# Gate products written to PSUM in the order of their eviction, and one more low one-hot group on ACT

## The chip, the cores and the metric

The kernel runs on one core of a Trainium2 chip. Its engines work side by side and wait for each other by semaphores: PE (TensorE, matrix products into PSUM), ACT (ScalarE), DVE (VectorE), POOL (GpSimd), and SP, whose queue issues the DMA transfers between DRAM and SBUF. The metric is the time of one execution on the device in microseconds (us); what is compared is the median over several runs.

## The reference

A trunk of two layers over 256 latent tokens with 256 context tokens as a prefix, 1024 features. Each layer has an attention mixer and then an expert network, PEER, whose routing the change touches:

```python
def blk(xb):                                  # 128 tokens
    q = (xb @ wq).reshape(PEER_TBLOCK, PEER_HEADS, 2, PEER_DQ // 2)
    s = jnp.einsum('thpd,pnd->thpn', q, sub_keys).astype(jnp.float32)
    sv, si = lax.top_k(s, PEER_TOPK)
    cand = (sv[:, :, 0, :, None] + sv[:, :, 1, None, :]).reshape(...)
    cidx = (si[:, :, 0, :, None] * PEER_NKEYS + si[:, :, 1, None, :]).reshape(...)
    fv, fp = lax.top_k(cand, PEER_TOPK)
    eidx = jnp.take_along_axis(cidx, fp, axis=-1)
    g = jax.nn.softmax(fv, axis=-1)
    ue = jnp.take(u, eidx, axis=0)
    ve = jnp.take(v, eidx, axis=0)
    a = jnp.einsum('thkd,td->thk', ue, xb).astype(jnp.float32)
    wgt = (jax.nn.gelu(a, approximate=False) * g).astype(xb.dtype)
    return jnp.einsum('thk,thkd->td', wgt, ve)
```

Each token has 8 heads with 16 experts each, so 128 pairs (i, j) of half keys with a gate g; the expert is 128 i + j of 16384.

## The kernel before

**Dense experts.** For most token blocks (three of four in layer 0, two of two in layer 1) the kernel does not gather rows. It goes through all 16384 experts in 128 chunks: `achunk` forms the activations of one chunk for all tokens (a product of the tokens with u, split in a high and a low part, lines 191 to 193, or in plain float32, line 213; then Gelu on ACT, line 1023, into a ring buffer), `weight` multiplies them with the gates (line 1151), and `fchunk` multiplies the result with v. For this the gates must lie as a dense matrix G[i, j, token], zero where a token does not choose an expert. `gates` builds it, and it is `gates` that the change touches.

**Building G.** For one token the 128 x 128 matrix of gates is a product of two one-hot matrices over its 128 choices: `oh` (choice k has j) and `og` (choice k has i, times its gate). Per block of 128 tokens there are 16 builds of 8 tokens, so 48 builds in layer 0 and 32 in layer 1. One build does the following.

- DVE writes both one-hot matrices in float16 (line 930, `oh`).
- The gate goes into `og` as a high and a low float16 part. The high part is one DVE instruction (line 933). The low part has four groups of two tokens: the first `d = 4 - AGRP` groups are one DVE instruction (line 936), of the others each token is one ACT activation of 128 columns (line 940). With `AGRP = (2,)` it is two groups on DVE, and 4 activations.
- GPIPE = 2 builds later PE forms the products (line 954): 8 tokens, two products each (high and low part, accumulated), in two PSUM tiles `p` of four tokens.
- ACT copies each tile, scaled, to `stage` (line 957), the eviction. `stage` holds 32 tokens in the order [i, token], so that the token is innermost. The tile in PSUM lies as [token, i]: the eviction reads it in a row and writes each word 32 words (128 bytes) behind the last.
- After every fourth build SP writes `stage` to G in DRAM (two transfers, line 961). When all is written, `load_g` reads G back in pieces for the main loop (line 1139).

**The order.** The code is a set of generators: `prologue` steps through the routing and the builds, and between steps `peer` puts in chunks of `achunk`, 27 ahead in layer 0 and 47 in layer 1 (`LAG`), and in layer 0 pieces of the next layer's modulation vectors (`filler`; weights of line 162, products of line 245). The tile layer then orders the instructions of each engine by its own reckoning of when they can start; on the chip each engine runs its list in order. The stages that hold the builds I call the gate stages.

Of the kernel before, what the change touches and what calls it, by code (L numbers as in the profile page):

```python
# [34 lines left out]
KLAG = 3  # L35
AGRP = (2,)
YLAG = (3, 3)
# [38 lines left out]
class Phase:  # L76
    """a pool whose tags have a set number of buffers"""

# [12 lines left out]
class Kernel:  # L91
# [32 lines left out]

# [1 line left out]
    def start_weights(self):  # L126
# [60 lines left out]

# [1 line left out]
    def mm3(self, out, lh, ll, rh, rl, start, stop):  # L189
# [5 lines left out]
    def proj_t(self, key, hh, hl, c=512, **kw):  # L195
        """[128 columns, c tokens] in PSUM"""
        if key in self.pre:
            return self.pre.pop(key)
        w = self.take(key, **kw)
        p = self.ps()  # L200
        if not isinstance(w, tuple):
            self.product8(p[:, :c], w)
            return p
        wh, wl = w
        for k in range(8):
            b = slice(k * 128, (k + 1) * 128)
            self.mm3(p[:, :c], wh[:, b], wl[:, b], hh[:, k, :c], hl[:, k, :c], k == 0, k == 7)
        return p

    def product8(self, out, w):  # L210
        """the same in float32, of the modulated norm kept whole"""
        for k in range(8):
            self.nc.tensor.matmul(out, w[:, k * 128:(k + 1) * 128], self.h32[:, k, :], start=k == 0, stop=k == 7)  # L213

    def proj_n(self, name, hh, hl, width, nt=4):
        """natural layout: nt banks [128 tokens, width]"""
        ps = [self.ps() for _ in range(nt)]
        for b in range(4):
            wh, wl = self.take((name, b))
            for q in range(2):  # L220
                c = slice(q * width, (q + 1) * width)
                for t in range(nt):
                    tt = slice(t * 128, (t + 1) * 128)
                    self.mm3(ps[t][:, :width], hh[:, 2 * b + q, tt], hl[:, 2 * b + q, tt],
                             wh[:, c], wl[:, c], b == 0 and q == 0, b == 3 and q == 1)
        return ps
# [3 lines left out]

# [1 line left out]
    def ada_mm(self, l, v, half, pool):  # L232
        """half of one modulation vector for both conditions, in rows 0 and 1 of each 32 as four partial sums"""
        nc = self.nc
# [69 lines left out]

# [1 line left out]
    def rstd(self, ss, n, width):  # L306
# [7 lines left out]
    def squares(self, x, half, ss, junk):  # L314
        """sum of squares of one half of a token block; with the second the factor of the norm"""
        self.nc.scalar.activation(junk, x[:, half * 512:half * 512 + 512], AF.Square, accum_out=ss[:, half:half + 1])
        if half:
            s = self.small([128, 1], "ss1")
            self.nc.vector.tensor_tensor(s, ss[:, 0:1], ss[:, 1:2], op=OP.add)
            return self.rstd(s, 1, D)  # L320

    def norm_mod(self, xs, rst, l, vsh, vsc, keys, mid=None):
        """modulated norm, transposed; the projections of keys go along with it"""
        nc = self.nc
# [51 lines left out]
    def rope(self, x, p, perm, cos, sin, n):  # L376
        """x [128, n] from p in PSUM, its first 256 columns (the latents) rotated, the rotation after the next one"""
        self.nc.scalar.copy(x[:, :n], p[:, :n])
        self.rope_end()
        self.roping = (x, perm, cos, sin)  # L380
# [13 lines left out]

# [1 line left out]
    def out_proj(self, l, yh, yl, src, T):  # L396
# [38 lines left out]

# [1 line left out]
    def probs1(self, P, S, scale, sink=None, bias=None):  # L437
        """P [128, 2, nk] <- exp of the two heads' scores less their maximum; sums in sm"""
        nc = self.nc
# [30 lines left out]
    def flip(self, x, nk, eng):  # L470
        """[128, 128 nk] -> [128 keys, nk, 128]"""
        p = self.ps([128, nk, 128])
        for k in range(nk):
            self.transpose(p[:, k, :], x[:, k * 128:(k + 1) * 128])
        t = self.m.t("PT", [128, nk, 128])
        if eng:
            self.nc.vector.tensor_copy(t, p)
        else:
            self.nc.scalar.copy(t, p)
        return t  # L480

# [1 line left out]
    def mixer0(self, xs, sq):  # L483
# [99 lines left out]

# [1 line left out]
    def mixer1(self, xs, sq):  # L585
# [9 lines left out]
        self.rope(kr, self.proj_t(("cdin", 0), hh, hl), *r32, 512)  # L595
        # cq | ckv in natural layout
        ckv = self.proj_n("ckv", hh, hl, 384)
# [36 lines left out]
        nc.vector.tensor_tensor(kvl, kf, kvh.bitcast(F), op=OP.subtract)  # L634
        # kr (replicated), dq, dk transposed
        dq, dk = [], []
# [13 lines left out]
        for t, p in enumerate(self.proj_n("dv", hh, hl, 512)):  # L650
            self.rope_end()
            nc.scalar.copy(dv[t // 2][:, t % 2, :], p)
        # latent queries, keys and values
        wh, wl = self.take(("uq", 0))
# [121 lines left out]

# [1 line left out]
    def top16(self, V, X, a, b):  # L778
        """sorted top 16 of each a, b as scratch, interleaved over the lists"""
        nc = self.nc  # L780
# [11 lines left out]
    def route_scores(self, l, T, nd, hh, hl):  # L792
        """sorted top 16 of each half key for the dense blocks; scores of a further block go to DRAM"""
        nc = self.nc
# [43 lines left out]
    def route(self, sv, al):  # L838
        """experts i, j and gates of one token block; a generator, leaves them in self.rt"""
        nc = self.nc  # L840
# [63 lines left out]
    def gates(self, go, ti, G):  # L904
        """gate matrix of 128 tokens -> DRAM; a generator"""
        nc = self.nc
# [36 lines left out]
        def product():  # L943
# [5 lines left out]
            for half in range(2):  # L949
                p = self.ps([128, 4, 128])  # L950
                for k in range(4):
                    for w in range(2):
                        g, b = half * 2 + k // 2, k % 2
                        nc.tensor.matmul(p[:, k, :], oh[:, 0, g, :, b], og_[:, w, g, :, b], start=(w == 0),  # L954
                                         stop=(w == 1))
                c4 = q * 8 + half * 4
                nc.scalar.activation(stage[:, :, c4:c4 + 4].rearrange("p i t -> p t i"), p, AF.Copy,  # L957
                                     scale=1.0 / GSCALE)
            if q == 3:
# [12 lines left out]
    def peer(self, l, xs, sq, nd):  # L972
        """nd dense token blocks; a further block, if any, goes by gathered rows; returns the pieces of f"""
        nc = self.nc
# [49 lines left out]

        # routing and gate matrix, with the first products of the main loop in between
        def prologue():
# [71 lines left out]
        def gather(n0, n1, after=None):  # L1098
            """rows of slots n0..n1, not before after is there"""
            n1 = min(n1, 256)  # L1100
# [69 lines left out]
        def pace(j):  # L1170
            """slots used by the end of iteration j, even in time"""
            def at(i):
                return i + min(i, NCH - lag)
            return min(256, -(-256 * (at(j + 1) - at(LATE)) // (at(NCH - 3) - at(LATE))))
# [28 lines left out]
    def residual(self, l, f):  # L1203
        """x + g2 f, in a new mixer phase"""
        nc = self.nc
# [27 lines left out]
    def run(self):  # L1233
# [34 lines left out]
        nc.vector.tensor_scalar(self.nsink, self.pk("sink"), -1.0, None, op0=OP.mult)  # L1268
        # lambda of the differential heads, gain of its norm
        lv = self.const([128, 2], name="lv")  # L1270
# [28 lines left out]
        xs, sq = self.residual(1, f)  # L1299
        # final norm  # L1300
        fg = self.m.t("q4", [128, 1024], name="fg")
# [16 lines left out]

# [1 line left out]
def rope_table(dim):  # L1320
    """cos and sin of the axial rotation for one head of dim features, [dim, 256 positions]"""
    half = dim // 4
# [11 lines left out]
def rope_perm(dim):  # L1334
    """lhsT of the product that gives (-x2, x1) for each quarter pair, over 128 partitions"""
    q = dim // 4
# [8 lines left out]
def col_blocks(w):  # L1345
    """[1024, 128 n] -> [n, 128 rows of a block, 8 blocks * 128 columns]"""
    k, n = w.shape
    return np.ascontiguousarray(w.reshape(8, 128, n // 128, 128).transpose(2, 1, 0, 3)).reshape(n // 128, 128, 1024)


def row_pairs(w):
    """[1024, n] -> [4, 128, 2 * n]"""
    k, n = w.shape
# [3 lines left out]
def layout(x, c, ctx, c_ctx, ada_w, ada_b, norm1_g, norm2_g, w_out, peer_wq, peer_keys, peer_u, peer_v,  # L1357
# [55 lines left out]
    z["na_bias"] = nb  # L1413
    # layer 0 projections
    w = ab_w_in[0]
    pair = np.concatenate([np.concatenate([np.arange(64) + 64 * h, np.arange(64) + 64 * (h + 4)]) for h in range(4)])
    z["ab_in"] = col_blocks(np.concatenate([w[:, 0:1024], w[:, 1536 + pair], w[:, 2048:2304]], 1))
    z["ab_v"] = row_pairs(w[:, 1024:1536])
    # layer 1 projections
    w = cd_w_in[0]  # L1420
# [39 lines left out]
```

## Time and profile before

| | us |
|---|---|
| runs of the kernel before, median of 3 | 2739.52 |
| their lowest and highest | 2731.03, 2754.28 |
| the profiled execution, span from first to last instruction | 2734.2 |
| TensorE busy in it | 2610.7 |
| ACT busy in it | 1267.3 |

The profile is of one execution. For it the span is the time that is known, and nothing is known of what lies around it; it is within the range of the three runs, 5.3 us under their median. A busy engine in the profile is one that has an instruction in flight; products on TensorE overlap each other, so that a busy TensorE need not be a full one.

### The profile page before, as it was taken

The numbers are of one execution on the slowest core, as the hardware profiler recorded it, in microseconds if no ns is written. First come the engines' busy times: TensorE is split into PE (matmuls) and PEld (weight loads), VectorE is DVE, ScalarE is ACT, GpSimd is POOL, SyncE is SP. The second block draws the span as 40 slices with busy tenths as digits, with TensorE's granted clock in tenths as the row PEclk, the third lists the DMA queues.
The fourth block names the chain that finished last, engine by engine and source line by source line (L and its number), as shares of the span: only waits on it lengthen the run. The fifth ranks groups of instructions, "written<-read, shape, count | busy, mean of one in ns | idle before, by whom it ended". The sixth has DMA issues, their size and how long they took to land.

```text
span 2734.2 us, 43073 instructions
## 1 busy us (share of the span) xinstructions
PE 2610.7 (95%) x16265; PEld 2261.8 (83%) x16265; DVE 1876.3 (69%) x3862; ACT 1267.3 (46%) x2201; POOL 529.2 (19%) x534
## 2 busy tenths in 40 slices
PE   7999998989999999999999989998999999999998
PEld 6866787878899999999899767757999899999986
DVE  4267588886977777777777765365997565555455
ACT  3255335997333333333333333343499444444454
POOL 0000000000045555566565530000000000000000
PEclk9999999999999999999999998998999999999999
DMA  7262323977688888888888862453467976565355
GB/s 291 101 216 86 111 88 128 287 235 246 232 313 311 308 315 306 316 299 321 294 309 288 275 225 75 164 195 113 144 215 242 318 267 210 208 211 214 130 193 183
DMA packets 240977, 614.15 MB, mean 225 GB/s; under 512 B 18384, under 2 KB 102608, under 8 KB 240768
## 3 DMA queue, kind: packets, MB, share of 16 engines
q1 hardware_dynamic: 203904, 477.17, 50.6%
q0 software_dynamic: 36864, 134.23, 13.9%
q8 instruction: 127, 2.08, 0.3%
q14 instruction: 82, 0.67, 0.1%
HBM read 558.90 MB, written 52.43 MB: 224 GB/s over the span
## 4 chain that ended last, share of the span: by engine, by line
PE 62%; DVE 6%; DMA 3%; ACT 3%; issue 2%; POOL 1%; SPq 0%; DVEq 0%; POOLq 0%; ACTq 0%
PE p L192 19%; PE p L191 19%; PE p L193 19%; DMA gr<-in_v,ix 1%; PE p L213 1%; PE s L707 1%; PE p L229 1%; DVE ws L168 1%; ACT stage L957 1%; ACT og L940 1%; DVE vs L168 1%; DMA sc<-sd 1%; PE p L954 1%; ACT ws L167 1%; PE p L245 0%
## 5 line engine op out<-in xcount | busy, mean ns | idle before, releaser
L167 ACT CAST ws<-w 128x1024 fp32r<-128x1024 f32 (+1 forms) x327 | 343.0, 1050 | 634.0 <-PE p L192 581.4
L168 DVE TENSOR_TENSOR ws<-w,ws 128x1024 fp32r<-128x1024 f32 (+1 forms) x327 | 397.5, 1216 | 267.7 <-ACT ws L167 267.4
L192 PE MATMUL p<-vs,w 128*128 128x512 f32 x1280 | 502.2, 393 | 7.5 <-DVE vs L168 7.5
L167 ACT CAST vs<-v 128x1024 fp32r<-128x1024 f32 x256 | 269.5, 1053 | 509.5 <-PE p L192 509.5
L191 PE MATMUL p<-vs,w 128*128 128x512 f32 x1280 | 499.6, 391 | 4.4 <-ACT vs L167 4.4
L193 PE MATMUL p<-vs,w 128*128 128x512 f32 x1280 | 501.6, 392 | 0.0
L191 PE MATMUL p<-hh,ws 128*128 128x384 f32 (+2 forms) x1336 | 472.2, 354 | 6.2 <-ACT ws L167 2.9
L193 PE MATMUL p<-hh,ws 128*128 128x384 f32 (+2 forms) x1336 | 466.0, 349 | 1.5 <-DVE ws L168 1.5
L192 PE MATMUL p<-hl,ws 128*128 128x384 f32 (+2 forms) x1336 | 466.6, 349 | 0.0
L168 DVE TENSOR_TENSOR vs<-v,vs 128x1024 fp32r<-128x1024 f32 x256 | 312.8, 1222 | 152.7 <-ACT vs L167 151.0
L191 PE MATMUL p<-hp,ws 128*128 128x256 f32 x1032 | 295.5, 287 | 1.8 <-ACT ws L167 1.1
L193 PE MATMUL p<-hp,ws 128*128 128x256 f32 x1032 | 292.8, 284 | 0.8 <-DVE ws L168 0.8
L192 PE MATMUL p<-hp,ws 128*128 128x256 f32 x1032 | 293.2, 284 | 0.0
L192 PEld LDWEIGHTS p<-vs,w 128*128 128x128 f32 x1280 | 241.3, 189 | 56.5 <-DVE vs L168 11.1
L193 PEld LDWEIGHTS p<-vs,w 128*128 128x128 f32 x1280 | 240.9, 188 | 53.7 <-DVE w L1153 3.0
L191 PEld LDWEIGHTS p<-vs,w 128*128 128x128 f32 x1280 | 241.1, 189 | 50.6 <-ACT vs L167 4.6
L191 PEld LDWEIGHTS p<-hh,ws 128*128 128x128 f32 x1336 | 255.0, 191 | 24.7 <-ACT ws L167 4.3
L192 PEld LDWEIGHTS p<-hl,ws 128*128 128x128 f32 x1336 | 254.6, 191 | 14.9 <-issue 0.5
L193 PEld LDWEIGHTS p<-hh,ws 128*128 128x128 f32 x1336 | 254.5, 190 | 13.1 <-DVE ws L168 2.0
L1123 DVE SCALAR_TENSOR_TENSOR acc<-gr,ga,acc 128x1024 f32<-128x1024 f32 x128 | 164.2, 1283 | 102.3 <-DMA gr<-in_v,ix 101.7
L1118 DVE SCALAR_TENSOR_TENSOR gr<-gr,hn 128x1024 f32<-128x1024 f32 x128 | 156.2, 1224 | 108.5 <-DMA gr<-in_u,ix 102.5
L311 POOL TENSOR_TENSOR rso<-rsm,mhalf 128x1 f32<-128x1 f32 x30 | 20.1, 671 | 1079.4 <-DVE rsm L309 1079.4
(267 smaller groups left out, 4127.6 us busy)
## 6 DMA issues: line engine op xcount, KB each, us to landing
w<-in_uT SPq DMA_DIRECT2D x256, 512.0 KB
v<-in_v SPq DMA_DIRECT2D x256, 512.0 KB
w<-in_ada_w SPq DMA_DIRECT2D x96, 512.0 KB
G<-stage SPq DMA_DIRECT2D x40, 1024.0 KB
g<-G SPq DMA_DIRECT2D x32, 768.0 KB
w<-in_wq SPq DMA_DIRECT2D x32, 512.0 KB
g<-G SPq DMA_DIRECT2D x32, 512.0 KB
w<-in_w_out SPq DMA_DIRECT2D x16, 512.0 KB
```

The lines of the kernel that those rows point to most:

```text
L167: self.nc.scalar.copy(hi, raw)
L168: self.nc.vector.tensor_tensor(lo, raw, hi.bitcast(F), op=OP.subtract)
L191: m(out, lh, rh, start=start, stop=False)
L192: m(out, lh, rl, start=False, stop=False)
L193: m(out, ll, rh, start=False, stop=stop)
L213: self.nc.tensor.matmul(out, w[:, k * 128:(k + 1) * 128], self.h32[:, k, :], start=k == 0, stop=k == 7)
L229: self.nc.tensor.transpose(out, x, self.ck("ident"))
L707: nc.tensor.matmul(S[:, s, :], a[c][h, q], b[c][h, :], start=True, stop=kind == "d", tile_position=(64 * s, 0))
L940: nc.scalar.activation(og_[:, 1, g, :, b], oh[:, 1, g, :, b], AF.Copy, scale=gl[:, k:k + 1])
L954: nc.tensor.matmul(p[:, k, :], oh[:, 0, g, :, b], og_[:, w, g, :, b], start=(w == 0), stop=(w == 1))
L1118: nc.vector.scalar_tensor_tensor(t, t, 1.0, hn, op0=OP.mult, op1=OP.mult, accum_out=ga[:, 0, n:n + 1])
L1123: nc.vector.scalar_tensor_tensor(acc, t, ga[:, 0, n - 128:n - 127], acc, op0=OP.mult, op1=OP.add)
```

## The change

`AGRP` goes from 2 to 3: of the four low groups of a build three are on ACT (6 activations) and one on DVE (128x256 in place of 128x512). The PSUM tile `p` changes its order from [token, i] to [i, token]: each product writes its 128 words four words apart, four tokens lie interleaved, and the eviction reads PSUM in a row and writes runs of four words to `stage`, one run each 128 bytes. The rest of the diff takes out comments and moves lines behind 957 up by one.

```diff
-AGRP = (2,)
+AGRP = (3,)
...
             for half in range(2):
-                p = self.ps([128, 4, 128])
+                p = self.ps([128, 128, 4])
                 for k in range(4):
                     for w in range(2):
                         g, b = half * 2 + k // 2, k % 2
-                        nc.tensor.matmul(p[:, k, :], oh[:, 0, g, :, b], og_[:, w, g, :, b], start=(w == 0),
+                        nc.tensor.matmul(p[:, :, k], oh[:, 0, g, :, b], og_[:, w, g, :, b], start=(w == 0),
                                          stop=(w == 1))
                 c4 = q * 8 + half * 4
-                nc.scalar.activation(stage[:, :, c4:c4 + 4].rearrange("p i t -> p t i"), p, AF.Copy,
-                                     scale=1.0 / GSCALE)
+                nc.scalar.activation(stage[:, :, c4:c4 + 4], p, AF.Copy, scale=1.0 / GSCALE)
```

**ACT at the end of layer 0's gate stage.** The rows are the last activations for `og`, the evictions to `stage`, the high halves of weight casts (`ws`, line 167) and the Gelu into `ring`. Before:

```order
L940 ACTIVATE og<-oh,gl 128x128 x4
L957 ACTIVATE stage<-p 128x4x128
L167 CAST ws<-w 128x1024
L1023 ACTIVATE ring<-p 128x384
L940 ACTIVATE og<-oh,gl 128x128 x4
L957 ACTIVATE stage<-p 128x4x128 x6
L167 CAST ws<-w 128x1024 x2
```

Now:

```order
L940 ACTIVATE og<-oh,gl 128x128 x6
L957 ACTIVATE stage<-p 128x128x4 x2
L167 CAST ws<-w 128x1024
L1022 ACTIVATE ring<-p 128x384
L940 ACTIVATE og<-oh,gl 128x128 x6
L957 ACTIVATE stage<-p 128x128x4 x6
L167 CAST ws<-w 128x1024
```

Each build has six activations in place of four, and at the end six evictions still stand ahead of the casts for the last chunks.

**SP in the middle of layer 0's gate stage.** The rows are the loads of u for the chunks (`w<-in_uT`) and the writes of G, one pair for each `stage`. Before:

```order
L998 DMA w<-in_uT 128x1024 x3
L961 DMA G_4081<-stage 128x16x128 x2
L998 DMA w<-in_uT 128x1024 x4
L961 DMA G_4081<-stage 128x16x128 x2
L998 DMA w<-in_uT 128x1024 x4
L961 DMA G_4081<-stage 128x16x128 x2
```

Now:

```order
L997 DMA w<-in_uT 128x1024 x4
L960 DMA G_4081<-stage 128x16x128 x2
L997 DMA w<-in_uT 128x1024 x3
L960 DMA G_4081<-stage 128x16x128 x2
L997 DMA w<-in_uT 128x1024 x4
L960 DMA G_4081<-stage 128x16x128 x4
```

One load of u stands ahead of a write of G that it stood behind, and one pair of writes stands ahead of a load.

## Rows read from the trace of the kernel before

**Rows 1.** The page's head and its first part, whole span

```profile
span 2734.2 us, 43073 instructions
...
PE 2610.7 (95%) x16265; PEld 2261.8 (83%) x16265; DVE 1876.3 (69%) x3862; ACT 1267.3 (46%) x2201; POOL 529.2 (19%) x534
```

**Rows 2.** Busy us (x instructions) by stretch: PE, PEld, DVE, ACT, POOL, PEclk, DMA, GB/s

```profile
453.00:545.00 92.00, 85.88 (x885) 74.94 (x878) 80.96 (x215) 81.81 (x158) 1.58 (x3) 0.96 0.77 248
545.00:592.00 47.00, 40.64 (x356) 37.95 (x355) 40.62 (x69) 44.23 (x80) 0.53 (x1) 0.89 0.85 266
592.00:648.00 56.00, 45.26 (x387) 40.85 (x385) 38.96 (x53) 54.65 (x110) 0.00 (x0) 0.91 0.64 182
1977.00:2055.00 78.00, 78.00 (x726) 75.59 (x725) 71.01 (x165) 72.04 (x133) 0.00 (x0) 1.00 0.71 222
2055.00:2128.00 73.00, 69.81 (x661) 66.67 (x659) 52.05 (x64) 69.77 (x135) 0.00 (x0) 1.00 0.79 247
```

**Rows 3.** Timeline of PE in layer 0's stage: start, us, what

```profile
571.48 0.33 PE L193 MATMUL p<-hh,ws 128*128 128x384 f32 x1
571.65 0.33 PE L191 MATMUL p<-hh,ws 128*128 128x384 f32 x1
...
572.17 1.10 PE L954 MATMUL p<-og,oh 128*128 128x128 f16 x16
...
580.02 1.98 PE L954 MATMUL p<-og,oh 128*128 128x128 f16 x16 [3.47 <-DVE og L933]
```

**Rows 4.** Chain that ended last, layer 1's stage: start, us, what

```profile
2023.62 3.46 PE p L213 x16
...
2030.91 0.94 PE p L954 x16
...
2099.49 1.86 ACT stage L957 x2
```

**Rows 5.** Groups on PE, 453 to 648: busy us, mean ns, idle before

```profile
L191 PE MATMUL p<-hh,ws 128*128 128x384 f32 x169 | 61.6, 365 | 2.6 <-ACT ws L167 2.6
L954 PE MATMUL p<-og,oh 128*128 128x128 f16 x768 | 59.5, 226 | 17.4 <-DVE og L933 9.2 <-ACT og L940 7.2 <-DVE og L936 0.3
```

**Rows 6.** Timeline of PE in layer 1's stage

```profile
1995.22 0.28 PE L193 MATMUL p<-hp,ws 128*128 128x256 f32 x1
1995.34 0.28 PE L191 MATMUL p<-hp,ws 128*128 128x256 f32 x1
```

**Rows 7.** Groups on PE, 1977 to 2128

```profile
L192 PE MATMUL p<-hp,ws 128*128 128x256 f32 x249 | 70.4, 283 | 0.0
...
L213 PE MATMUL p<-h,w 128*128 128x256 f32 x121 | 27.8, 382 | 0.6 <-ACT ring L1023 0.6
```

**Rows 8.** Groups on ACT, 453 to 648

```profile
L957 ACT ACTIVATE stage<-p 128x512 f32<-128x512 f32 x96 | 97.8, 1131 | 1.7 <-PE p L954 1.7
L940 ACT ACTIVATE og<-oh,gl 128x128 f16<-128x128 f16 x192 | 62.5, 438 | 0.8 <-DVE oh L930 0.7
...
L261 ACT COPY gbo<-p 128x512 f32<-128x512 f32 x4 | 2.4, 610 | 0.0
```

**Rows 9.** Groups of all engines, 455 to 860, two of DVE

```profile
L936 DVE TENSOR_TENSOR og<-oh,ijgt 128x512 f16<-128x512 f16 x48 | 20.1, 418 | 0.0
...
L899 DVE TENSOR_TENSOR e<-e 128x256 f16<-128x256 f16 x6 | 1.7, 290 | 0.0
```

**Rows 10.** Stretch of the group at 580.02, columns as in Rows 2

```profile
580.10:581.70 1.60, 1.60 (x16) 1.50 (x17) 1.60 (x3) 1.43 (x5) 0.00 (x0) 0.50 1.05 289
```

**Rows 11.** Timeline of all engines, end of layer 0's stage

```profile
640.65 5.71 ACT L957 ACTIVATE stage<-p 128x512 f32<-128x512 f32 x6
...
647.26 0.44 PE L191 MATMUL p<-hh,ws 128*128 128x384 f32 x1 [1.93 <-ACT ws L167]
```

**Rows 12.** Timeline of SP, end of layer 1's stage

```profile
2122.77 3.39 SPq L961 DMA_DIRECT2D G<-stage  x2
...
2130.39 0.48 SPq L1139 DMA_DIRECT2D g<-G  x1
```

## The prediction

> **What bounds the kernel now.** I read the page's first part to see which engine is full, then the stretches of the two gate stages, then the groups of instructions there, and last the chain and the timelines, for what is waited for. Over the whole span TensorE is the busy engine, 2610.7 of 2734.2 us [rows 1], but the change touches only the two stages in which the gate matrix is built, 453 to 648 us in layer 0 and 1977 to 2128 us in layer 1, and the five stretches there say something else [rows 2]. In layer 0 (first three stretches) ACT is busy 81.81 + 44.23 + 54.65 = 180.7 of 195 us, TensorE 171.8, and TensorE's granted clock is below full in all three: ACT is the limit and TensorE has room. How much room, the busy column hides, since a matmul's shown duration overlaps the next one's. Starts of the 384-column products stand 0.17 us apart [rows 3], and a gate group of sixteen takes 0.94 us of the chain [rows 4]. With some 507 of the former (169 on each of three lines) and 48 x 16 of the latter [rows 5], that is 87 + 45 us, and with some 11 us for the small products, an estimate, TensorE needs 143 of the 195 us. So 52 us of room, part of it spent at the half clock.
>
> Layer 1 is different. In its first stretch TensorE is busy 78.00 of 78.00 us at full clock, in the second 69.81 of 73 [rows 2]. Counted by issue: some 747 products of 256 columns (249 on each of three lines) at 0.12 us between starts and 121 float32 products at 3.46 / 16 = 0.22 us [rows 4, 6, 7], with 32 x 0.94 us of gate products, make 146 of 151 us. TensorE is the limit there; only in part of the second stretch does the chain go over ACT's evictions (1.86 us for two [rows 4]), and some 5 us of TensorE's time are free.
>
> **The eviction** (line 957) runs 160 times. In layer 0's stage it takes 97.8 us for 96, 1.02 us each in a row and 1.13 alone; it writes one word at a time, 128 bytes apart. The copy of the same 128x512 float32 from PSUM that writes in a row takes 0.61 us [rows 8]. No row shows runs of four words, so the new eviction lies between 0.5 us (0.61 less the 0.11 by which neighbours overlap) and 1.02. I take 0.5 to 0.6, since the four words stand side by side and the scattered write pays at each word. [...]
>
> **The low one-hot product** moves two activations per build from DVE to ACT. An activation of line 940 costs 62.5 / 192 = 0.326 us [rows 8], so ACT gets 0.65 us more. DVE's line 936 shrinks from 128x512 to 128x256, 0.418 to 0.290 us by the row of line 899 of the same type [rows 9]: 0.13 us less per build, 6 us in layer 0, off the path, because DVE there is less busy than ACT.
>
> ACT per build is thus 2 x (1.02 - 0.5 to 0.6) = 0.84 to 1.04 us less and 0.65 more: 0.2 to 0.4 us less, 10 to 19 us over layer 0's 48 builds, 6 to 13 over layer 1's 32. The new order on ACT is the old one with six for four. SP's order exchanges some loads and G writes; its queue is the same in length, and I cost it at nothing. If that cover fails, one G write that SP holds until its eviction is done delays the u loads behind it by the time of one or two evictions, 1 to 2 us.
>
> **The strided product.** No TensorE write in this trace leaves words out. The bounds: nothing, 0.94 us of issue for sixteen as now; and, above, a write that is slowed as ACT's scattered write is, 1.02 against 0.5 to 0.6 us, a factor of 1.7 to 2. A gate group at half the clock is a row of just that rate: 1.98 us for sixteen in place of 1.10, first start to last end [rows 3], the granted clock 0.50 [rows 10]. That is 0.88 us more per build. I take this end, because the only write of lone words that the trace prices runs at about half rate, and a product at full rate delivers 128 words in 0.94 / 16 = 0.059 us, far faster than ACT's 512 in 0.6. It costs 48 x 0.88 = 42 us of TensorE in layer 0 and 28 us in layer 1.
>
> [...]
>
> **The sum.** Layer 0: ACT falls from 181 to 162 to 171 us, TensorE rises from 143 to 185, so TensorE takes over as the fullest engine. Today the stage lasts 14 us longer than its fullest engine is busy; with the same surplus it would take 199 us, 4 more. Its end gets better: six evictions, 5.71 us, stand at the end of the stage ahead of the casts that TensorE waits for (it idles until 647.26) [rows 11], and they become 3 to 3.5, some 2.5 us less. Together +1 us, between -9 (the surplus goes, since the clock no longer falls) and +8. Layer 1: 146 + 28 = 174 us of issue against 151 us now, +23; the relief on ACT is worth nothing once TensorE is the limit throughout. After the stage's last chunks TensorE waits for the first load of G, issued at 2130.39, behind the last write of G, issued from 2122.77 [rows 12]. That write waits for the last evictions; the last four, at 0.4 to 0.5 us less each, bring it forward by 2 us. Layer 1: +21, between +14 and +27. All else, the main loops above all, is unchanged.
>
> That is +22 us on a profiled span of 2734.2. The median of the three runs shown, 2739.52, is 5.3 us above that span, and the span lies inside their 2731 to 2754; I put the sum on the median and drop a microsecond for layer 0's wider downside: **2760 us**, 0.8% slower, which counts as no change: less than 1% is what a measurement of this kernel can hardly tell.
>
> **Rivals.**
> A. Half-rate strided products, as above: 2760 (2744 to 2776). For it: the scattered write on ACT. Against: that is another engine and another memory.
> B. TensorE writes strided at full rate. Then only ACT's relief counts: layer 0 -10 to -19 and 2.5 at its end, layer 1 only the 3 to 5 us of its second stretch and 2 at its end: -17 to -28, most likely -20, 2720. For it: nothing in the trace shows TensorE bound by its output. [...]
> C. The strided write costs more than half rate, since the second product of each pair also has to read and add at each lone word. This is the rival on the slow side. By the sums above, x us more per build cost 48x - 40 in layer 0 and 32x - 7 in layer 1. At a third of the rate x is 1.88: +50 and +53, 2843; at a quarter 2.82: +95 and +83, 2918. It decides from x = 0.93 on, where 80x - 47 is 1% of the time: that is hardly more than A's 0.88, so A and C part near a factor of two.
> D. The eviction does not do what it is meant to: runs of four words are no cheaper than lone ones (or PSUM reads were its limit). It breaks even at 1.02 - 0.33 = 0.69 us. At 1.02, ACT gets 31 us more in layer 0 and 21 in layer 1, where it then needs 163 of what were 151 us: +31 and +12 to +21, about +45, 2785, before any cost on TensorE. Against: the copies at 0.61 us read PSUM just as wide.
>
> **How the numbers follow.** A 0.45, B 0.32, C 0.17, D 0.06. In A, seven in ten of its times are within 1% (27 us) and the rest above. In B, one in eight is faster by over 1%. C and D are slower. So faster 0.05, within 1% 0.60, slower 0.35. The range has to reach down over B (2714) and up over A and D (2800); C, beyond, is what is left out, with a few in the hundred below. A's own range is 2744 to 2776, and it alone would be too narrow, since B lies on the other side.
>
> **What would show it.** In the profile of the changed kernel: line 954's sixteen from 1.10 to about 1.98 us at a granted clock of 1.00 (A), the same 1.10 (B), 3 us and more (C). The eviction at 0.5 to 0.6 us and 480 activations of line 940 at 0.33 (against D: above 0.69). ACT in layer 0's stage down to 162 to 171 us. The length of the two stages: layer 0 within 10 us of 195, layer 1 about 174 against 151 us (A), or 175 to 185 and 145 to 148 (B). The prediction is wrong if the product's pace stays, or if it falls to a third; or if layer 0, with both engines near full, waits on both in turn and loses 20 us more.

## The result, and the profile after

The changed kernel takes 2768.94 us (median of 7 runs, 2758.86 to 2779.76), the kernel before 2740.61 (7 runs): a ratio of 1.009, 95% interval 1.0067 to 1.0113. That is 28 us or 0.9% slower; 2760 was forecast, and the time lies in the range of 2714 to 2800.

The page's head and first part of the changed kernel, against [rows 1]:

```profile
span 2761.7 us, 43240 instructions
...
PE 2656.8 (96%) x16265; PEld 2310.8 (84%) x16265; DVE 1869.4 (68%) x3862; ACT 1255.2 (45%) x2361; POOL 534.4 (19%) x534
```

ACT has 160 instructions more and 12 us less to do. TensorE has as many instructions as before and is busy 46 us longer. The two gate stages, in stretches as in [rows 2] (the last three begin or end later, since the stages are longer):

```profile
453.00:545.00 92.00, 90.41 (x796) 82.21 (x789) 74.77 (x208) 75.34 (x192) 1.58 (x3) 0.99 0.74 236
545.00:592.00 47.00, 43.82 (x381) 40.60 (x380) 41.06 (x74) 39.36 (x94) 0.53 (x1) 1.00 0.78 243
592.00:652.00 60.00, 57.25 (x432) 53.30 (x432) 39.59 (x56) 55.52 (x154) 0.00 (x0) 1.00 0.68 203
1989.00:2070.00 81.00, 81.00 (x646) 78.64 (x645) 68.22 (x164) 64.88 (x156) 0.00 (x0) 1.00 0.64 198
2070.00:2152.00 82.00, 81.54 (x665) 78.77 (x663) 48.46 (x63) 67.32 (x169) 0.00 (x0) 1.00 0.71 220
```

In layer 0 ACT was the fullest engine; now TensorE is, 191 of 199 us against 170 of ACT, and its clock hardly falls (0.99 to 1.00). In layer 1 TensorE has hardly a gap left. One gate group of sixteen, in the timeline of PE, against 1.10 us in [rows 3] (the granted clock over both is 1.00):

```profile
505.14 1.92 PE L954 MATMUL p<-og,oh 128*128 128x128 f16 x16
```

The groups on ACT from 453 to 653 us, against [rows 8]:

```profile
L940 ACT ACTIVATE og<-oh,gl 128x128 f16<-128x128 f16 x288 | 91.9, 447 | 5.9 <-DVE oh L930 4.9 <-PE p L954 0.5 <-ACT ws L167 0.4
L957 ACT ACTIVATE stage<-p 128x512 f32<-128x512 f32 x96 | 54.5, 604 | 10.0 <-PE p L954 9.9
```

The eviction fell from 1.02 to 54.5 / 96 = 0.57 us each. It now waits for the product (9.9 us in all, before 1.7). The chain that ended last, over layer 1's stage (1990 to 2180 us), names the gate products first and no line of ACT:

```profile
by line: PE p L954 28.7%; PE p L193 18.6%; PE p L192 18.4%; PE p L191 18.3%; PE p L213 14.6%; DVE ws L168 0.6%; issue 0.6%; PE p L229 0.2%; DVE oh L930 0.0%
```

Where the 27.5 us between the two spans come from can be read from the timelines at five marks: the first and the last product of the main loop of each layer (`p<-vs,w`), and the first one-hot build of layer 1. Each row starts where the row above it ends.

| stretch of the profiled runs | before, us | after, us | difference |
|---|---|---|---|
| start to layer 0's main loop | 0 to 668.0 | 0 to 673.9 | +5.9 |
| layer 0's main loop, first to last product | 668.0 to 1626.8 | 673.9 to 1638.0 | +5.3 |
| from there to the first build of layer 1 | 1626.8 to 1974.6 | 1638.0 to 1986.4 | +0.6 |
| from there to layer 1's main loop | 1974.6 to 2139.9 | 1986.4 to 2169.0 | +17.3 |
| layer 1's main loop, first to last product | 2139.9 to 2721.8 | 2169.0 to 2749.3 | -1.6 |

### The profile page after: what moved, and what is told of

Read it like the earlier page. It is cut to its first block, busy times and chain, and to the rows that moved or that the text cites. A ratio compares the mean times of both kernels' runs of the same rounds, so it can differ in the third digit from the quotient of the medians.

```text
span 2761.7 us, 43240 instructions
## 1 busy us (share of the span) xinstructions
PE 2656.8 (96%) x16265; PEld 2310.8 (84%) x16265; DVE 1869.4 (68%) x3862; ACT 1255.2 (45%) x2361; POOL 534.4 (19%) x534
## 4 chain that ended last, share of the span: by engine, by line
PE 85%; DVE 8%; DMA 3%; ACT 1%; issue 1%; POOL 1%; SPq 0%; DVEq 0%; POOLq 0%; ACTq 0%
PE p L192 23%; PE p L191 23%; PE p L193 23%; PE p L954 5%; PE p L229 2%; PE p L245 1%; PE s L527 1%; PE p L213 1%; DVE ws L168 1%; PE p L560 1%; PE s L707 1%; DMA gr<-in_v,ix 1%; DMA w<-in_ada_w 1%; DVE sv L784 1%; DVE sv L790 1%
## 5 line engine op out<-in xcount | busy, mean ns | idle before, releaser
L192 PE MATMUL p<-vs,w 128*128 128x512 f32 x1280 | 502.4, 393 | 11.4 <-DVE vs L168 11.4
L192 PEld LDWEIGHTS p<-vs,w 128*128 128x128 f32 x1280 | 241.3, 189 | 60.4 <-DVE vs L168 15.2
```

What stands on the lines that cost most here:

```text
L192: m(out, lh, rl, start=False, stop=False)
```

## The experiments

The theory (S) was that the strided product at half rate makes the whole loss, and that the eviction gains what the prediction gave it. The rivals were that the third ACT group has a share in it (R), and, for a remedy, that ACT would pay for reading PSUM scattered as it pays for writing SBUF scattered (P). The first four kernels ran on one chip with the kernel before at 2739.08 us, the last three on another with the kernel before at 2740.67 us; each ratio is to the kernel before on the same chip.

**e1_agrp3**: the kernel before with the third group on ACT alone.

```diff
-AGRP = (2,)
+AGRP = (3,)
```

Expected: 

> The kernel before with three of four low groups on ACT, the product and the eviction as before. Theory S (the strided product's half rate is the whole loss): ACT gets 0.65 us more per build and the eviction stays at 1.02 us, so ACT needs 212 us of layer 0's stage (195 before) and 163 of layer 1's (151 before); 2770 to 2785, sixteen products at 1.10 us. Rival R (the third ACT group costs little, since ACT's list has gaps): 2740 to 2755.

Measured: 2777.76 us, ratio 1.0138 (1.0104 to 1.0172). The eviction stays slow (1.02 us each), and ACT is busy 205.98 of 213 us in layer 0's stage. By itself the move costs 39 us, so S's numbers hold and R's don't; rival D of the prediction had priced it at 45.

```profile
453.00:666.00 213.00, 183.19 (x1630) 157.87 (x1620) 155.28 (x337) 205.98 (x440) 2.10 (x4) 0.90 0.69 213
```

**e2_stride4_agrp2**: the changed kernel with two groups on ACT again.

```diff
-AGRP = (3,)
+AGRP = (2,)
```

Expected: 

> The changed kernel with two of four low groups on ACT again; product strided, eviction in runs of four. Theory S: TensorE is the limit in both gate stages whatever ACT does, so 2762 to 2770, within 0.3% of the changed kernel; sixteen products at about 1.9 us, ACT in layer 0's stage down by another 30 us. Rival R (the third ACT group makes part of the loss): 2745 to 2758.

Measured: 2757.34 us, ratio 1.0075 (1.0051 to 1.0099), 5 us under what S gave and at the upper edge of R's span. Its interval overlaps the changed kernel's. TensorE is busy 196.16 of 200 us with ACT down at 148.04, so freeing ACT further brings layer 0's stage little: its main loop begins at 670.1, 3.8 us before the changed kernel's, and layer 1's stage is as long in both. Whether the third group costs nothing here or some 4 to 12 us (the profiles' 3.8, the medians' 11.6), these intervals can't tell; R isn't ruled out for the changed kernel, and the price that S gives the product rests on the next two runs.

```profile
453.00:653.00 200.00, 196.16 (x1634) 183.38 (x1627) 162.81 (x338) 148.04 (x347) 2.10 (x4) 0.99 0.75 232
```

**e3_psumread4_agrp3** and **e4_psumread4_agrp2**: the kernel before, its product as it was; ACT takes over the change of order, by reading PSUM 512 bytes from word to word, the four tokens in turn. The first also has `AGRP = (3,)`, the second keeps `AGRP = (2,)`.

```diff
-                nc.scalar.activation(stage[:, :, c4:c4 + 4].rearrange("p i t -> p t i"), p, AF.Copy,
+                nc.scalar.activation(stage[:, :, c4:c4 + 4], p.rearrange("p t i -> p i t"), AF.Copy,
                                      scale=1.0 / GSCALE)
```

Expected of the first: 

> Products written in a row as in the kernel before; the eviction reads PSUM four tokens apart (512 bytes) and writes runs of four words; three of four low groups on ACT. Theory S: the product is back at 1.10 us for sixteen; if ACT reads PSUM scattered at no cost, the eviction takes 0.57 us as in the changed kernel, ACT needs 168 us in layer 0's stage, and the time is 2712 to 2728. Rival P (a scattered read of PSUM costs ACT as much as a scattered write): the eviction stays at about 1.0 us and the time is that of the kernel before with three groups on ACT, 2770 to 2785.

Expected of the second: 

> As the run before it, with two of four low groups on ACT. Theory S with a free read: ACT falls from 181 to some 137 us in layer 0's stage, where DVE (160 us busy) or the waits between engines then set the end: 2705 to 2722. Rival P: 2735 to 2745, the kernel before.

Measured: 2729.62 us, ratio 0.996 (0.9936 to 0.9983), and 2710.62 us, ratio 0.9899 (0.9864 to 0.9934). The first is 2 us above the 2712 to 2728 that S gave, the second inside S's range. The groups on ACT of the first and then of the second, whole span:

```profile
L957 ACT ACTIVATE stage<-p 128x512 f32<-128x512 f32 x160 | 87.8, 610 | 3.9 <-PE p L954 3.6
```

```profile
L957 ACT ACTIVATE stage<-p 128x512 f32<-128x512 f32 x160 | 86.6, 597 | 6.1 <-PE p L954 4.3 <-DMA G<-stage 1.3
```

87.8 and 86.6 us for 160 are 0.55 and 0.54 us each: the scattered read is free, and P falls. With the eviction as fast as in the changed kernel and in e2 (0.57 us in both), these two differ from them in the product's pace: 2729.62 against 2768.94 us with three groups on ACT, 2710.62 against 2757.34 with two. The strided product thus costs 39 and 47 us (with three groups 36 by the ratios, since the changed kernel was timed in another series), and the eviction in runs of four by itself gains 28 us over the kernel before. From the kernel before to the changed one the medians thus go down 28 us with the eviction, up 47 with the product and up 12 with the third group, the last not clear of the noise. e4 beats both kernels. In its layer 0 no engine stands out any more:

```profile
453.00:637.00 184.00, 165.81 (x1656) 151.15 (x1657) 167.66 (x354) 146.10 (x349) 2.11 (x4) 0.95 0.82 252
1960.00:2104.00 144.00, 144.00 (x1360) 139.65 (x1360) 123.30 (x231) 115.15 (x267) 0.00 (x0) 0.99 0.80 247
```

Three more ask what it is in the strided write that costs: a word that stands alone (L), the step or its size (D), or the adding at such words (A).

**e5_stride2**: two tokens interleaved in place of four, three groups on ACT; the edit is against the kernel before.

```diff
-AGRP = (2,)
+AGRP = (3,)
...
-                p = self.ps([128, 4, 128])
+                p = self.ps([128, 2, 128, 2])
...
-                        nc.tensor.matmul(p[:, k, :], oh[:, 0, g, :, b], og_[:, w, g, :, b], start=(w == 0),
+                        nc.tensor.matmul(p[:, k // 2, :, k % 2], oh[:, 0, g, :, b], og_[:, w, g, :, b], start=(w == 0),
...
-                nc.scalar.activation(stage[:, :, c4:c4 + 4].rearrange("p i t -> p t i"), p, AF.Copy,
+                nc.scalar.activation(stage[:, :, c4:c4 + 4].rearrange("p i (a t) -> p a i t", a=2), p, AF.Copy,
```

Expected: 

> Products that write every second word (two tokens interleaved), eviction that reads PSUM in a row and writes runs of two words, three of four low groups on ACT. If a lone word is what costs (theory L), sixteen products take as long as with every fourth word, 109 ns from start to start, and the time is that of the changed kernel or above; if the distance counts (theory D), the pace lies between 58 and 109 ns. The eviction: 0.57 us if two words in a run are enough for the full rate, up to 1.02 if not; at 0.57 the time is 2762 to 2772, at 1.02 2790 to 2810.

Measured: 2769.74 us, ratio 1.0102 (1.0066 to 1.0139): the changed kernel's time. Its timeline of PE shows the changed kernel's pace, and its evictions, in runs of two words, take 94.9 / 160 = 0.59 us:

```profile
509.56 1.92 PE L954 MATMUL p<-og,oh 128*128 128x128 f16 x16
```

```profile
L957 ACT ACTIVATE stage<-p 128x512 f32<-128x512 f32 x160 | 94.9, 627 | 14.6 <-PE p L954 14.3
```

**e6_no_accumulate**: the changed kernel with no product that adds.

```diff
-                        nc.tensor.matmul(p[:, :, k], oh[:, 0, g, :, b], og_[:, w, g, :, b], start=(w == 0),
-                                         stop=(w == 1))
+                        nc.tensor.matmul(p[:, :, k], oh[:, 0, g, :, b], og_[:, w, g, :, b], start=True, stop=True)
```

Expected: 

> The changed kernel in which the second product of each pair starts anew and overwrites the first, so that no product adds to what is in PSUM (the high parts of the gates are left out of the result). If the half rate comes from writing lone words (theory L), all products stay at 109 ns from start to start; if it comes from reading and adding at lone words (theory A), they go at 57 to 60 ns, or, if only the first of a pair was fast before, the mean falls.

Measured: one run, 2757.7 us, and the same pace. A falls:

```profile
505.78 1.92 PE L954 MATMUL p<-og,oh 128*128 128x128 f16 x16
```

**e7_runs_of_two**: as many words in as many products, written as runs of two.

```diff
-                        nc.tensor.matmul(p[:, :, k], oh[:, 0, g, :, b], og_[:, w, g, :, b], start=(w == 0),
-                                         stop=(w == 1))
+                        o, s = 64 * (k % 2), 2 * (k // 2)
+                        nc.tensor.matmul(p[:, o:o + 64, s:s + 2], oh[:, 0, g, :, b], og_[:, w, g, :, b],
+                                         start=(w == 0), stop=(w == 1))
```

Expected: 

> The changed kernel in which each product writes 64 runs of two words, four words apart, in place of 128 lone words (the gates land at other places of the tile, so the output is another). Theory L: two words that stand together are written at the full rate, 57 to 60 ns from start to start, and the time falls to 2715 to 2732. Theory D (any step in the output's pattern costs): 109 ns and 2762 to 2772, or a pace between.

Measured: one run, 2735.21 us; that is 3 us above what L gave, and inside the runs of e3 (2720.66 to 2742.78), whose ACT work and product pace it shares (the 160 evictions take 87.3 against 87.8 us, the products of layer 0 225 against 228 ns each). The pace is the full one, though the pattern has a step of four words:

```profile
500.34 1.10 PE L955 MATMUL p<-og,oh 128*128 128x128 f16 x16
```

L holds: words that stand alone cost 0.82 us per sixteen products, two words apart as well as four, adding or not; two words side by side cost nothing more. The pairs of e7 all begin at an even word; whether pairs that begin at an odd word are as fast, no run shows.

## Why the prediction was right, and where its sizes were off

**The price of the strided product** was bounded by nothing and by ACT's scattered write, and taken at a group at half the clock, +0.88 us per build. Measured +0.82 (1.92 against 1.10 us, both at a granted clock of 1.00), near that row. Rivals B and C fall with it. That lone words are slow came as argued; that the factor came out so near is partly luck, since the two rows it was taken from are another engine's write and a clock that had fallen, and neither is what happened here. Nor does every pattern with gaps cost: e7's pairs stand four words apart and run at 1.10 us. Words in pairs are enough there, each pair beginning at an even word.

**The eviction** was put at 0.5 to 0.6 us and measured 0.57 us; rival D falls. That the scattered write pays at each word was my estimate; e5's runs of two words take 0.59 us against 1.02 for lone words, so nearly the whole gain comes with the second word of a run.

**The low groups**: 91.9 / 288 = 0.319 us per activation (0.326 forecast). Per build ACT has 0.9 us less for evictions and 0.64 more for `og`; in layer 0's three stretches it is busy 170 us, the forecast's 162 to 171. That the gain is not seen, because TensorE takes over as the fullest engine, came as argued; e3 shows it, where the same ACT work with the fast product is 39 us faster.

**Layer 1**: +21 forecast, +17.3 measured. Up to the last gate product (2117.4 us before, 2151.0 now) the stage is 21.8 us longer. The +23 of the forecast becomes 21 by the price alone, since each of 32 builds is 0.06 us cheaper. The end was under-sized: I took 2 us off for the last evictions, and it is 4.5 us shorter. Before, the main loop's first product came after a wait of 4.41 us for ACT's cast, which itself stood behind the load of G that the prediction named (DVE waited 7.98 us for that load, ACT 6.78 us for DVE). Now TensorE is busy throughout that end, 18.00 of 18.00 us from 2151 to 2169, and the wait is gone. The kernel before, in the timeline of PE, and the changed kernel in the columns of [rows 2]:

```profile
2139.90 1.05 PE L191 MATMUL p<-vs,w 128*128 128x512 f32 x2 [4.41 <-ACT vs L167]
```

```profile
2160.00:2170.00 10.00, 10.00 (x69) 9.36 (x68) 5.31 (x9) 5.35 (x9) 0.00 (x0) 1.00 1.02 371
```

**Layer 0**: +1 forecast, +5.9 measured, inside its bounds of -9 to +8. The stage's last product comes at 652.0 us, 199 us after 453, as reckoned, but that it came out is luck, since the reckoning mixes two marks. The surplus of 14 us over the fullest engine was taken up to 648 us, behind the old stage's last eviction (it ended at 646.4). Up to the last product (640.9) the old stage was 188 us long, only 7 over ACT's 181, while the new one is 14 over the reckoned 185. What failed is this term, and with it the account of the end, from which I took 2.5 us off. The last product came 11 us later, not 4; of these 5 came back, since the main loop begins 21.9 us after it (652.0 to 673.9), not 27.1 (640.9 to 668.0). In that end TensorE waited (busy 24.84 of 27.10 us), and its clock had fallen (0.94); now it is busy throughout, at 1.00. The kernel before, and then the changed kernel:

```profile
640.90:668.00 27.10, 24.84 (x138) 24.18 (x138) 12.24 (x14) 16.57 (x22) 0.00 (x0) 0.94 0.92 302
```

```profile
652.10:673.90 21.80, 21.80 (x135) 21.80 (x133) 12.43 (x15) 11.93 (x17) 0.00 (x0) 1.00 0.94 320
```

**Not forecast**: the +5.3 us in layer 0's main loop, whose code the change leaves alone. From first to last product it is 958.8 us before and 964.1 after. In e1 to e7, in order, it is 956.2, 964.1, 960.7, 960.4, 968.9, 959.6 and 968.9. It scatters by 13 us over these kernels, without order in what they change: e6, strided as the changed kernel is, is at 959.6, and e7, at the full pace, at 968.9. What goes with it is one wait of TensorE, for the low part of v (line 168, ahead of line 192): 7.5 us before and 11.4 after, 5.6 in e1, where the loop is shortest, 8.5 to 9.3 in e2, e3, e4 and e6, and 14.4 and 15.2 in e5 and e7, where it is longest. I count the +5.3 as scatter of single profiled runs; what makes that wait longer was not tried and stays open. Without it the profiled runs differ by 22 us, the sum of the prediction, in which layer 1 was set 4 us too high and layer 0 5 us too low; so the sum fits because two misses cancel. The medians differ by 28 us where 20.5 was forecast (2760 against 2739.52), with an interval of 18 to 31 us, so the runs don't show that the loop's part is all scatter.

## What to carry to other kernels

Where an operand must change its order on the way from the product to SBUF, let the engine that reads PSUM do it, with the scattered side on its read: here the read was free (0.54 to 0.55 us per eviction against 0.57 in a row), a write of lone words to SBUF nearly doubled the eviction (1.02 against 0.57 us), and a write of lone words by TensorE nearly halved the product's pace (1.92 against 1.10 us for sixteen). A change that speeds one engine at the cost of another is judged stage by stage: the 0.8 us per build that TensorE got were mostly hidden in layer 0, where it had room (39 us more of products, 5.9 us more of time), and counted for two thirds in layer 1, where it had little (26 us and 17.3 us). And move work to an engine only after the relief that is to make room for it has been measured with all that it costs: the third group on ACT made e3 19 us slower than e4, although its eviction was as fast (0.55 against 0.54 us).

## What the runs showed that was not expected

- Sixteen products that write 128 lone words each take 1.92 us in place of 1.10, 0.05 us more for each product, whether the words are two or four apart and whether the product adds to them or not; 64 runs of two words, four words from run to run and each at an even word, go at the full pace.
- ACT reads PSUM 512 bytes apart at no cost: 0.54 to 0.55 us per 128x512 eviction against 0.57 in a row.
- ACT's write to SBUF needs a run of only two words for nearly the full pace: 0.59 us for runs of two, 0.57 for four, 1.02 for lone words 128 bytes apart.
